# Modulation parts of a layer gathered in one PSUM bank and transposed together, ahead of attention and convolution

## The chip, the cores and the metric

One core of a Trainium2 chip runs the whole program. The metric is the device time of one execution in microseconds (us). The core has TensorE for matmuls (PE in the profile; PEld is its load of the stationary operand), VectorE (DVE), ScalarE (ACT), GpSimd (POOL) and SyncE (SP), whose queue issues the weight DMAs. TensorE writes into PSUM, eight banks of 128 partitions x 512 fp32 values.

## The reference, cut to what matters

Two transformer blocks run one after the other on 256 tokens of width 1024. The first has two layers (differential attention beside a depthwise convolution, then a feed-forward part), with 16 meta tokens ahead of the 256. The second has a gated delta rule beside dilated attention, then a mixture of 64 experts, and is modulated by a vector `c`:

```python
cs = jax.nn.silu(c)                                   # (1, 1024)
mod = (cs @ w_ada[l] + b_ada[l])[:, None, :]          # (1, 1, 6144)
sh1, sc1, gt1, sh2, sc2, gt2 = jnp.split(mod, 6, axis=-1)
h = _rms(x, g_mix[l]) * (1.0 + sc1) + sh1             # ahead of the second block's mixer
```

`mod` depends on `c` alone, so the kernel computes it during the first block. `w_ada` is 1024 x 6144 fp32, 24 MB.

## The kernel before, in words

Activations lie with features on partitions and tokens along the free axis. Dense weights pass through `weights()` (L153): a block of 1024 x 256 fp32 (1 MB) goes by one SyncE DMA into `raw`, a ring of three buffers shared by all dense weights. For the precise matmuls it is split into a high and a low fp32r part, `hi` by ScalarE (L165) and `lo` by VectorE (L166), and `mm3` (L168) issues three matmuls (L172 to L174). The modulation weights are used unsplit, straight from `raw`.

A layer of the first block (`first_block`) projects the convolution input, queries and keys, then takes the steps that the string `ORDER[l]` lists, one letter each: `s` scores and softmax (L420 to L431), `v` values (L540 to L545), `a` attention (L453 to L478), `c` convolution, `p` modulation parts, `n` channel norm (L507 to L527), `w` a block of w_out. The string is the order in which the program writes the work down. A planner with a timeline of its own then fixes each engine's order ahead of the run: earlier steps have precedence, but a later step's instruction goes first where the planner sees the earlier ones waiting. Weight DMAs and splits get a higher precedence by `PRI`. Within an engine the fixed order is kept on the chip, and SyncE issues the weight blocks in the order in which they are written down.

The convolution has 31 taps for each of four channel groups. `TAPS` gives some of them to TensorE as matmuls with a diagonal that ScalarE writes (L487, L488), 31 taps of group 0 and 16 of group 1 in layer 0, and 16 of group 0 in layer 1. ScalarE reads that sum out of PSUM (L489) and VectorE adds the other taps (L501). The channel norm needs all four groups and yields the convolution half of `cat`, of which L527 writes the last piece. The projection by w_out first sums the attention half for `AHEAD` = 5 output blocks into five banks, then the convolution half.

PSUM banks come in three kinds: `mm` and `ax` with three buffers each and `dx` with two. The convolution sums and the modulation parts use `dx`.

The modulation is cut into 24 parts of 256 columns: 12 in layer 0, 10 in layer 1 and 2 (with weights loaded ahead into `wada`) at the end of layer 1. A part (`ada_parts`, L622) takes a `dx` bank and forms eight products, one per 128 features, with `cs` broadcast to 32 columns as stationary (L630). Their column groups run side by side: product k goes to partitions 32 (k mod 4) and on. Each fp32 product is two matmuls in the trace. ScalarE copies the 128 x 256 result (L633), two more products with a column of 1/32 turn each half into one column (L635), and VectorE adds the bias into `mod` (L636).

Of the kernel before, what the change touches and what calls it, by code (L numbers as in the profile page):

```python
# [9 lines left out]
F32 = mybir.dt.float32  # L10
# [3 lines left out]
OP = mybir.AluOpType  # L14
# [4 lines left out]
KC = D // 128  # L19
# [9 lines left out]
TAPS = (((0, 31), (1, 16)), ((0, 16),))  # L29
AHEAD = 5  # L30
PR0 = 9
ORDER = ("svacpnwwww", "svacpnwwww")


GQ, GK, GV, GZ, GB, DQ, DK, DV, GA, GBB = 0, 1024, 2048, 3072, 4096, 4112, 5648, 7184, 8720, 9744
# [74 lines left out]
class K:  # L110
# [197 lines left out]
    def first_block(s):  # L308
        nc, I, V, A, PE, SP, ap, cp = s.nc, s.I, s.V, s.A, s.PE, s.SP, s.ap, s.cp
        C, ident = dict(s.C), s.C["ident"]  # L310
# [8 lines left out]
        for k in range(KC):  # L319
            p = s.ax()  # L320
# [8 lines left out]
        for l in range(2):  # L329
# [42 lines left out]
            for i, (t0, n) in enumerate(((tq, nq), (0, T))):  # L372
# [3 lines left out]
                for b in range(2):  # L376
                    w = s.weights(w_in, 0, 8, 512 * i + 256 * b)
# [9 lines left out]
            q, k = qk  # L387
# [160 lines left out]
            wo = []  # L548
            for step in ORDER[l]:
                if step == "a":  # L550
# [11 lines left out]
                else:  # L562
                    s.ada_parts(ADA[l])
            h1 = s.hp.tile([128, KC, T], F32, name="h", bufs=2)
            ps = [(s.mm, s.mm, s.mm, s.dx, s.dx, s.ax)[j]() for j in range(AHEAD)]
            for j in range(AHEAD):
                for k_ in range(4):
                    s.mm3(ps[j], wo[j // 2], k_, 128 * (j % 2), cat, k_, tq, nq, k_ == 0, False)
# [30 lines left out]
            for b in range(4):  # L599
                ws = [(s.weights(I["w_down"][l], k0 * 128, nk, 256 * b), nk, k0) for k0, nk in ((0, 8), (8, 8), (16, 6))]  # L600
# [9 lines left out]
    def ada(s):  # L610

        I, V, A, ap = s.I, s.V, s.A, s.ap
        s.P2 = s.columns(ap, s.cp, (("b_ada_2", 48), ("c_2", 8), ("g_mix_2", 8), ("g_ffn_2", 8), ("final_g", 8),
                              ("gdn_norm_g_2", 1), ("dil_q_norm_g_2", 1), ("dil_k_norm_g_2", 1)), s.G, **s.scr)
        s.cs = s.cp.tile([128, KC], F32, name="cs")
        A.activation(s.cs, s.P2["c_2"], AF.Silu)
        s.sel = s.cp.tile([128, 1], F32, name="sel")
        V.memset(s.sel, 1.0 / 32)
        s.mod = s.cp.tile([128, 6, KC], F32, name="mod")
        s.nada = 0  # L620

    def ada_parts(s, n, ws=()):  # L622
        V, A, PE, ap = s.V, s.A, s.PE, s.ap
        mod = s.mod.rearrange("p a b -> p (a b)")
        for i in range(s.nada, s.nada + n):
            w = ws[i - s.nada] if ws else s.weights(s.I["w_ada_2"][0], 0, 8, 256 * i, False)
            p = s.dx()
            for k in range(KC):
                q = 32 * (k % 4)
                PE.matmul(p[q:q + 32, :256], s.cs[:, k:k + 1].to_broadcast([128, 32]), w[:, k],  # L630
                          start=(k < 4), stop=(k >= 4))
            row = ap.tile([128, 256], F32, name="adarow", **s.row)
            A.copy(row, p[:, :256])  # L633
            for j in range(2):
                PE.matmul(p[:, 256 + j:257 + j], row[:, 128 * j:128 * j + 128], s.sel, start=True, stop=True)  # L635
            V.tensor_tensor(mod[:, 2 * i:2 * i + 2], p[:, 256:258], s.P2["b_ada_2"][:, 2 * i:2 * i + 2], op=OP.add)  # L636
        s.nada += n

    def ada_ahead(s, n):

# [1053 lines left out]
```

## Time and profile before

| | us |
|---|---|
| median of 3 runs | 1670.66 |
| lowest and highest | 1669.35, 1672.37 |
| the profiled execution's own time | 1669.04 |
| its span in the trace | 1667.2 |

The profile is of one execution; its times are in us from the span's start. Layer 0's steps from scores to w_out lie at about 81 to 194 us, layer 1's at about 440 to 545, and the last two modulation parts at 735 to 741. The experts fill the time from about 1190 on. A busy TensorE may still run at a low clock: the column PEclk is the granted clock as a share of 2.4 GHz.

### The profile page before, as it was taken

What the parts mean: (1) busy time and instruction counts of PE and PEld (TensorE: products, weight loads), DVE (VectorE), ACT (ScalarE), POOL (GpSimd) and SP (SyncE); (2) the same over time, 40 slices, a digit from 0 to 9 for tenths busy, and PEclk for the clock granted to TensorE, in tenths of its full rate; (3) what the DMA queues carried; (4) which work ended last, traced back from release to release, by engine and by line L of the source; (5) the groups of instructions that cost most, each with busy time, mean ns of one, the idle gap of its engine ahead of it and who ended that gap; (6) DMA issues with size and microseconds to landing.
All of it is one profiled execution on the core that took longest, in us unless ns stands there. A gap on an engine that the chain in (4) does not pass through costs nothing.

```text
span 1667.2 us, 32866 instructions
## 1 busy us (share of the span) xinstructions
PE 1598.1 (96%) x13630; PEld 1358.0 (81%) x13630; DVE 865.5 (52%) x1764; ACT 744.5 (45%) x1492; POOL 14.4 (1%) x28
## 2 busy tenths in 40 slices
PE   7999999999999999989999999999899999999897
PEld 6966999999968999988999999999666576566463
DVE  6685766646987666458656654553422221222122
ACT  5376644445347544455856856643322211112121
POOL 2000000000000000000000000000000000000000
PEclk9999999999999999999999999999899999999999
DMA  8408655555466555754343342666799999999995
GB/s 249 140 26 274 194 179 174 172 172 174 130 203 192 176 189 171 234 167 140 114 128 102 102 129 89 233 191 223 285 365 421 420 419 420 420 420 420 420 420 243
DMA packets 209959, 389.29 MB, mean 234 GB/s; under 512 B 8855, under 2 KB 183313, under 8 KB 184977
## 3 DMA queue, kind: packets, MB, share of 16 engines
q1 hardware_dynamic: 209104, 386.66, 64.0%
q8 instruction: 108, 1.77, 0.5%
q0 software_dynamic: 704, 0.51, 0.3%
q14 instruction: 43, 0.34, 0.1%
HBM read 386.10 MB, written 1.05 MB: 232 GB/s over the span
## 4 chain that ended last, share of the span: by engine, by line
PE 76%; DMA 14%; ACT 5%; DVE 4%; issue 1%; SPq 0%; DVEq 0%; ACTq 0%
PE mm L172 14%; PE mm L173 14%; PE mm L174 14%; PE pm L1508 6%; DMA we<-in_w_exp_up 6%; PE pm L1534 4%; DMA we<-in_w_exp_down 3%; DMA we<-in_w_exp_gate 2%; PE pm L1472 2%; PE dx L488 2%; PE mm L195 2%; PE mm L196 1%; PE mm L197 1%; ACT hi L165 1%; DMA raw<-in_w_out 1%; PE dx L630 1%
## 5 line engine op out<-in xcount | busy, mean ns | idle before, releaser
L166 DVE TENSOR_TENSOR lo<-raw,hi 128x1024 fp32r<-128x1024 f32 (+2 forms) x300 | 347.9, 1192 | 144.2 <-ACT hi L165 142.9
L165 ACT CAST hi<-raw 128x1024 fp32r<-128x1024 f32 (+2 forms) x300 | 292.7, 1024 | 271.0 <-PE mm L173 150.5
L172 PE MATMUL mm<-xh,hi 128*128 128x272 f32 (+1 forms) x1008 | 288.1, 288 | 0.0
L173 PE MATMUL mm<-xl,hi 128*128 128x272 f32 (+1 forms) x1008 | 287.8, 286 | 0.0
L174 PE MATMUL mm<-xh,lo 128*128 128x272 f32 (+1 forms) x1008 | 286.6, 286 | 0.0
L1508 PE MATMUL pm<-we,xT 128*32 128x256 f32 (+2 forms) x2048 | 195.9, 392 | 8.4 <-DMA we<-in_w_exp_up 5.8
L173 PEld LDWEIGHTS mm<-xl,hi 128*128 128x128 f32 x1008 | 189.7, 188 | 0.9
L174 PEld LDWEIGHTS mm<-xh,lo 128*128 128x128 f32 x1008 | 189.4, 188 | 0.5
L172 PEld LDWEIGHTS mm<-xh,hi 128*128 128x128 f32 x1008 | 188.5, 188 | 0.7
L1508 PEld LDWEIGHTS pm<-we,xT 128*32 128x32 f32 (+2 forms) x2048 | 122.2, 129 | 76.0 <-DMA we<-in_w_exp_up 7.9
L173 PE MATMUL mm<-bigb,hi 128*128 128x256 f32 (+1 forms) x512 | 148.3, 290 | 0.1
L172 PE MATMUL mm<-hh,hi 128*128 128x256 f32 x384 | 110.6, 291 | 7.2 <-ACT hh L704 4.2
L1534 PE MATMUL pm<-we,hT 128*32 128x512 f32 (+2 forms) x512 | 112.5, 605 | 0.1
L173 PE MATMUL mm<-hl,hi 128*128 128x256 f32 x384 | 109.5, 286 | 0.7 <-DVE hl L705 0.7
L174 PE MATMUL mm<-hh,lo 128*128 128x256 f32 x384 | 108.4, 285 | 0.0
L1519 DVE SCALAR_TENSOR_TENSOR hp<-sil,cs,pm 128x256 f32<-128x256 f32 x26 | 17.6, 676 | 168.5 <-ACT sil L1517 168.5
L174 PE MATMUL mm<-biga,lo 128*128 128x272 f32 (+1 forms) x352 | 101.4, 288 | 0.0
L172 PE MATMUL mm<-biga,hi 128*128 128x272 f32 (+1 forms) x352 | 100.6, 286 | 0.0
L173 PEld LDWEIGHTS mm<-bigb,hi 128*128 128x128 f32 x512 | 97.5, 191 | 0.8 <-DVE bigb L478 0.3
L1539 DVE TENSOR_TENSOR y<-pm,gt 128x512 f32<-128x512 f32 x52 | 35.9, 689 | 119.5 <-PE pm L1534 119.5
L1517 ACT ACTIVATE sil<-pm 128x256 f32<-128x256 f32 x26 | 10.0, 384 | 175.2 <-PE pm L1508 175.2
L195 PE MATMUL mm<-hi,hh 128*128 128x256 f32 x288 | 85.8, 298 | 2.0 <-DVE cacc L861 2.0
(541 smaller groups left out, 3089.7 us busy)
## 6 DMA issues: line engine op xcount, KB each, us to landing
we<-in_w_exp_gate SPq DMA_DIRECT2D x64, 1024.0 KB, 19.6
we<-in_w_exp_up SPq DMA_DIRECT2D x64, 1024.0 KB, 19.8
we<-in_w_exp_down SPq DMA_DIRECT2D x64, 1024.0 KB, 19.7
raw<-in_w_in SPq DMA_DIRECT2D x62, 1024.0 KB, 5.3
raw<-in_w_gate_up SPq DMA_DIRECT2D x44, 1024.0 KB, 5.1
raw<-in_w_ada SPq DMA_DIRECT2D x22, 1024.0 KB, 6.0
raw<-in_w_down SPq DMA_DIRECT2D x16, 1024.0 KB, 5.1
raw<-in_w_out SPq DMA_DIRECT2D x12, 1024.0 KB, 6.7
```

What stands on the lines that cost most here:

```text
L165: s.A.copy(hi[:, a:b], raw[:, a:b])
L166: s.V.tensor_tensor(lo[:, a:b], raw[:, a:b], hi[:, a:b].bitcast(F32), op=OP.subtract)
L172: s.PE.matmul(ps[:, :n], a, xh, start=start, stop=False)
L173: s.PE.matmul(ps[:, :n], a, xl, start=False, stop=False)
L174: s.PE.matmul(ps[:, :n], b, xh, start=False, stop=stop)
L195: s.PE.matmul(p[:, :256], xh, w[0][:, k], start=(k == 0), stop=False)
L488: PE.matmul(p[:, :nq], dg, z[:, c, tq + j:tq + j + nq], start=(j == 0), stop=(j == n - 1))
L1472: s.PE.matmul(p[:, 256 * kk:256 * kk + 256], s.ht[h][:, i, k + kk], oh[:, i], start=(i == 0 and h == 0), stop=(i == 1 and h == 1))
L1508: mm = PE.matmul(gu[sg, 256 * m:256 * m + 256], xT[:, k, o + sg.start:o + sg.stop], w[m][:, k], start=(k == 0), stop=(k == 7))
L1519: V.scalar_tensor_tensor(hp.rearrange("p k q -> p q k"), sil.rearrange("p (q k) -> p q k", k=2), cs, gu[:, 256:].rearrange("p (q k) -> p q ...
L1534: PE.matmul(py[sg], hT[:, k, sg], w[2][:, k, 512 * j:512 * j + 512], start=(k == 0), stop=(k == 1))
L1539: V.tensor_tensor(y, py, s.gt2[:, 512 * j:512 * j + 512], op=OP.mult)
```

## The change: what it does

The order string puts the parts after the values and ahead of attention and convolution. All parts of one call of `ada_parts` go into the same columns of one bank. The stationary is now a 32-column window of a tile `one` that is zero except for its middle column, which holds `cs`: shifted by the part's number i, it puts the part's result in row i of each group of 32 partitions and adds zero to the other rows. After the last part the bank is copied once. Two products with `sel`, four stacked 32 x 32 identities, sum the four partition groups and transpose, so that column i holds part i, and one addition writes all parts of the call. One of the five banks of w_out's first sums changes from `dx` to `ax`.

```diff
-ORDER = ("svacpnwwww", "svacpnwwww")
+ORDER = ("svpacnwwww", "svpacnwwww")
...
-            ps = [(s.mm, s.mm, s.mm, s.dx, s.dx, s.ax)[j]() for j in range(AHEAD)]
+            ps = [(s.mm, s.mm, s.mm, s.dx, s.ax, s.ax)[j]() for j in range(AHEAD)]
...
-        s.sel = s.cp.tile([128, 1], F32, name="sel")
-        V.memset(s.sel, 1.0 / 32)
+        s.one = ap.tile([128, KC, 63], F32, name="one")
+        V.memset(s.one, 0.0)
+        A.copy(s.one[:, :, 31], s.cs)
+        s.sel = ap.tile([128, 32], F32, name="sel")
+        V.tensor_reduce(s.sel, s.C["ident"].rearrange("p (g i) -> p i g", g=4), axis=mybir.AxisListType.X, op=OP.add)
...
     def ada_parts(s, n, ws=()):
         V, A, PE, ap = s.V, s.A, s.PE, s.ap
-        mod = s.mod.rearrange("p a b -> p (a b)")
-        for i in range(s.nada, s.nada + n):
-            w = ws[i - s.nada] if ws else s.weights(s.I["w_ada_2"][0], 0, 8, 256 * i, False)
-            p = s.dx()
+        i0, i1 = s.nada, s.nada + n
+        p = s.dx()
+        for i in range(i0, i1):
+            w = ws[i - i0] if ws else s.weights(s.I["w_ada_2"][0], 0, 8, 256 * i, False)
             for k in range(KC):
                 q = 32 * (k % 4)
-                PE.matmul(p[q:q + 32, :256], s.cs[:, k:k + 1].to_broadcast([128, 32]), w[:, k],
-                          start=(k < 4), stop=(k >= 4))
-            row = ap.tile([128, 256], F32, name="adarow", **s.row)
-            A.copy(row, p[:, :256])
-            for j in range(2):
-                PE.matmul(p[:, 256 + j:257 + j], row[:, 128 * j:128 * j + 128], s.sel, start=True, stop=True)
-            V.tensor_tensor(mod[:, 2 * i:2 * i + 2], p[:, 256:258], s.P2["b_ada_2"][:, 2 * i:2 * i + 2], op=OP.add)
-        s.nada += n
+                PE.matmul(p[q:q + 32, :256], s.one[:, k, 31 - i:63 - i], w[:, k], start=(i == i0 and k < 4),
+                          stop=(i == i1 - 1 and k >= 4))
+        row = ap.tile([128, 256], F32, name="adarow", **s.row)
+        A.copy(row, p[:, :256])
+        for j in range(2):
+            PE.matmul(p[:, 256 + 32 * j:288 + 32 * j], row[:, 128 * j:128 * j + 128], s.sel, start=True, stop=True)
+        mod, bias = (t.rearrange("p (i j) -> p i j", j=2)[:, i0:i1]
+                     for t in (s.mod.rearrange("p a b -> p (a b)"), s.P2["b_ada_2"]))
+        V.tensor_tensor(mod, p[:, 256:320].rearrange("p (j i) -> p i j", j=2)[:, i0:i1], bias, op=OP.add)
+        s.nada = i1
```

## Rows read from the trace of the kernel before

**Rows 1.** The page's busy line: time, share of the span, instructions.

```profile
PE 1598.1 (96%) x13630; PEld 1358.0 (81%) x13630; DVE 865.5 (52%) x1764; ACT 744.5 (45%) x1492; POOL 14.4 (1%) x28
```

**Rows 2.** Stretches: length, busy PE, PEld, DVE, ACT, POOL, clock, DMA share, GB/s.

```profile
86.00:116.00 30.00, 30.00 (x131) 18.66 (x129) 25.16 (x111) 19.40 (x70) 0.00 (x0) 1.00 0.00 1
131.00:158.00 27.00, 26.71 (x238) 18.43 (x242) 15.20 (x41) 12.92 (x43) 0.00 (x0) 1.00 0.84 272
158.00:165.00 7.00, 4.77 (x41) 2.93 (x34) 3.07 (x9) 5.40 (x9) 0.00 (x0) 0.65 1.07 342
165.00:171.00 6.00, 6.00 (x28) 5.69 (x28) 5.68 (x8) 6.00 (x11) 0.00 (x0) 0.55 0.86 274
...
455.00:470.00 15.00, 15.00 (x109) 13.20 (x108) 14.16 (x48) 3.01 (x11) 0.00 (x0) 1.00 0.00 1
470.00:500.00 30.00, 26.57 (x250) 15.99 (x249) 24.51 (x99) 15.80 (x53) 1.10 (x2) 1.00 0.89 280
500.00:511.00 11.00, 9.69 (x49) 7.84 (x49) 9.13 (x14) 8.61 (x13) 0.00 (x0) 0.84 1.04 327
511.00:524.00 13.00, 10.66 (x75) 9.31 (x76) 8.80 (x18) 10.29 (x27) 0.00 (x0) 1.00 0.39 129
```

**Rows 3.** Waits of SyncE, 81 to 165 us: total, times, longest.

```profile
SPq L158 <- PE dx L630: 84.0, 11, 47.1
```

**Rows 4.** Chain of waits, both layers: start, length, what.

```profile
156.25 7.34 DMA raw<-in_w_out
...
498.59 9.92 DMA raw<-in_w_out
```

**Rows 5.** Tile `adarow`, the one-column matmuls: count, ns least/median/most, first and last start.

```profile
L635 PE MATMUL dx<-sel,adarow x96: 165/250/374, 120.2 to 740.4; 128*128 128x1 f32 x96
```

**Rows 6.** Timeline of TensorE, layer 0: start, length, what, idle before.

```profile
116.80 1.07 PE L630 MATMUL dx<-raw,cs 128*32 128x256 f32 x16
117.80 1.19 PE L488 MATMUL dx<-biga,dg 128*128 128x272 f32 x4
...
133.47 0.95 PE L635 MATMUL dx<-sel,adarow 128*128 128x1 f32 x8
...
135.76 2.98 PE L461 MATMUL mm<-biga,at 128*128 128x128 f32 x14
...
160.74 1.93 PE L630 MATMUL dx<-raw,cs 128*32 128x256 f32 x16 [1.99 <-DMA raw<-in_w_ada]
162.60 1.87 PE L635 MATMUL dx<-sel,adarow 128*128 128x1 f32 x8
164.71 0.59 PE L172 MATMUL mm<-bigb,hi 128*128 128x272 f32 x1 [0.24 <-ACT hi L165]
```

**Rows 7.** Timelines of ScalarE and VectorE in both layers, same columns.

```profile
83.52 0.21 ACT L616 ACTIVATE cs<-pc_b_ada 128x8 f32<-128x8 f32 x1
...
130.60 0.46 ACT L489 ACTIVATE biga<-dx,pc_norm_g 128x272 f32<-128x272 f32 x1
...
134.85 4.26 DVE L501 SCALAR_TENSOR_TENSOR biga<-biga,cw 128x272 f32<-128x272 f32 x8
...
167.67 0.43 DVE L527 SCALAR_TENSOR_TENSOR bigb<-biga,bigb 128x272 fp32r<-128x272 f32 x1
...
490.26 0.16 DVE L636 TENSOR_TENSOR mod<-dx,pc_b_ada 128x2 f32<-128x2 f32 x1 [2.23 <-PE dx L635]
...
500.48 0.47 DVE L501 SCALAR_TENSOR_TENSOR biga<-biga,cw 128x256 f32<-128x256 f32 x1
...
520.81 0.42 DVE L527 SCALAR_TENSOR_TENSOR bigb<-biga,bigb 128x256 fp32r<-128x256 f32 x1
```

**Rows 8.** Timeline of TensorE, layer 1, same columns.

```profile
441.65 0.62 PE L630 MATMUL dx<-raw,cs 128*32 128x256 f32 x2
...
451.88 0.64 PE L630 MATMUL dx<-raw,cs 128*32 128x256 f32 x8
...
471.64 0.63 PE L630 MATMUL dx<-raw,cs 128*32 128x256 f32 x6
```

## The prediction

> **What bounds the kernel now.** I read the page's busy line first: TensorE is busy for 96% of the span [rows 1], so a stage gets shorter if work leaves TensorE, if TensorE stops waiting, or if its clock rises. The table by stretch comes second [rows 2]. In layer 0, from 86 to 116 us, TensorE is busy all 30 us at full clock while DMA moves 1 GB/s; from 131 to 165 DMA runs at 272 to 342 GB/s, and TensorE falls to 4.77 us busy of 7 at clock 0.65, then 0.55. Layer 1 has the same shape: 1 GB/s from 455 to 470, 280 to 500, clock 0.84 from 500 to 511. So the 1 MB weight blocks stand still while there is room and crowd where the stage ends.
>
> Why they stand still is in the SyncE waits [rows 3]: the weight queue waited 84.0 us in all, once 47.1, for TensorE's modulation matmuls. The ring holds three blocks. The modulation parts are planned behind attention and convolution, so their blocks lie loaded and unused. The chain of waits shows the price: it passes through the landing of w_out blocks, 7.34 us in layer 0 and 9.92 in layer 1 [rows 4]. These come late because w_out follows the modulation blocks in one queue.
>
> **The change part by part.** *Transposes.* Each part now ends in two calls which are four matmuls of one column, because fp32 goes in two passes: 96 in all [rows 5]. Eight in a row, two parts, last 0.95 us [rows 6]; a length runs some 0.07 us into the next start (1.07 at 116.80, next at 117.80), so a part's four hold 0.44 us; I take 0.45, and 24 parts cost 10.8. Afterwards there are three groups, 12 matmuls. A 32-column form with this 128x128 stationary is not in the trace. From below the one-column slot bounds it, 0.11 us; from above the 128-column one, 0.21 (14 in 2.98 us at 135.76) [rows 6]. That is 1.3 to 2.5 us; I take 1.4, since the load of the stationary is the same as with one column. Saved: 9.4 us (8.3 to 9.5), as 4.9, 4.0 and 0.4 in layer 0, layer 1 and the last two parts. In the two layers TensorE is full around it, so it counts whole.
>
> *The rows.* The 16 matmuls of a part keep their number and shape; the stationary is a 32-column window of a zero tile instead of a broadcast column, same size, and I cost it at nothing. A part takes 1.00 us (116.80 to 117.80) [rows 6], 24.0 us before and after. On ScalarE 24 copies become 3, on VectorE 24 additions become 3. In layer 1 that also takes away stalls of VectorE: the addition at 490.26 waited 2.23 us with convolution taps queued behind it [rows 7].
>
> *The move.* The order of weight loads does not change: values, modulation, w_out. What changes is when a block is used up. `cs` exists at 83.5 us [rows 7], so the three loaded blocks can go from 85 to 88, and nine more stream through a ring that never stands still. At 272 GB/s for a share of 0.84 [rows 2] a full queue gives 324 GB/s, 3.2 us for 1.05 MB: nine take 29 us, and the last part runs at about 118 instead of 160.74 [rows 6]. Behind them SyncE issues w_out some 40 us before it does now, so neither w_out wait of [rows 4] should remain. The convolution's and the scores' matmuls move back by up to ten parts, 10 us, on TensorE.
>
> *What that gives at the stage's end.* In layer 0 the recoverable loss up to 171 us is: the 1.99 us DMA wait; the last part and its transposes at half speed (1.93 for 1.07, 1.87 for 0.95), 1.8 us; gaps of 0.29 us in the window from 131 and 0.24 at 164.71; and w_out's matmuls from 165 to 171 at clock 0.55 [rows 2, 6], 2.7 us. Together 7.0. Layer 1: idle 3.43 + 1.31 + 2.34 us of the three windows from 470 to 524, and 16% of 11 us of clock, 1.8; together 8.9 [rows 2]. I don't take all of it. With the modulation gone from the end, nothing fills TensorE between the steps of attention and of the channel norm. In layer 0 convolution taps on TensorE end at 130.6 (ScalarE starts reading the bank then), VectorE's at 139.1, and the first normed tile is ready at 168.1, 29 us later [rows 7]. Layer 1 needs 20 us for this chain (500.9 to 521.2) [rows 7]. If layer 0's taps slip by 10 us and its chain shrinks to 20, w_out's second half starts as late as now and most of the 7.0 is lost; if the chain shrinks further, most is kept. I take 4 of 7.0 in layer 0, and 3 of 8.9 in layer 1, where VectorE is busy 24.5 of 30 us from 470 to 500 [rows 2] and must now do w_out's casts amid its taps.
>
> *Fragments.* The planner fits a part's matmuls in between others. Two alone last 0.62 us, eight 0.64, six 0.63 [rows 8], 16 last 1.07 [rows 6]: a cut costs 0.1 to 0.5 us. Among the dense matmuls of queries and values more parts will be cut; eight cuts at 0.25 make 2 us lost (0 to 5, the upper end with ten cuts at 0.5).
>
> The Trainium skill, "TensorEngine Tiling (Array Packing)", section Key Properties, says that changing the tiling mode drains TensorE, where changing the tile within a mode doesn't. The 128x32 fragments agree: two cost as much as eight. By this rule alone the move only adds switches, and the sum would be the transposes' 9.4 less the fragments; by the stretch table it also gives back waits.
>
> *Additions.* A memset, one strided copy and one reduction, once, near 83 us; TensorE has the matmuls of the values and scores to do meanwhile, so nothing; uncovered it would be some 0.7 us, three times the 0.21 us that `cs` takes [rows 7]. The fifth partial sum of w_out moves to a bank of the three-bank kind, free by then: nothing.
>
> *Sum.* 9.4 + 4 + 3 - 2 = 14.4 us, off the profiled execution's 1669.04 (span 1667.2 and 1.8 around it). I shade it to 13.7, since the planner reorders everything around, so 1655.3; the median of the three runs lies 1.6 above the profiled one, and the prediction is **1657**. All that follows waits for the layers' results, the experts' loads too, since their buffers are those that the mixer frees; so the gain is carried to the end.
>
> **Rivals.** *A: only TensorE work is saved.* The stage ends wait on attention and channel norm instead of on DMA. For it: the chains of 29 and 20 us; against it: much of layer 0's chain is TensorE's queue filled with modulation parts. 9.4 less 2 to 4 us: 1664.
>
> *B: cut to pieces.* If all 22 parts are cut as layer 1's first is now (2, 8 and 6: 0.62 + 0.64 + 0.63, less 0.21 of overlap, for 1.00 [rows 8]), that costs 22 x 0.68 = 15 us and leaves 1 of the 16.4 us ahead of fragments: 1669. Against it: a part becomes ready all at once, when its block lands, and those of layer 0 run mostly whole now, as the 16 at 116.80 and 160.74 [rows 6].
>
> *C: the held bank (slower).* A group now holds one of only two `dx` banks from its first to its last part. In layer 0 the convolution's second channel group takes the same bank, so its 16 taps can't begin before the last addition has read it; then come 15 taps on VectorE (8 in 4.26 us [rows 7], so 8 us) and the chain. Today TensorE's taps end at 130.6. With layer 1's chain of 20 us they may end 9 us later before w_out's second half waits longer than now; since they take some 8 us themselves, it decides when the bank comes free later than about 131. A release at 150 puts their end at 158, VectorE's at 166, the first normed tile at 186 instead of 168: 18 us lost against 9.4 saved. If the planner leaves the parts spread as today, to 164 us, it is 32 us against 9.4: 1693. For it: the parts are paced by DMA, and fall behind the scores in order. Against it: 118 us as worked out above. I price it by the release at 150: 1679.
>
> *D: it does not move.* If planned starts stay where they were since SyncE's queue decides, only the transposes go: 1661, inside A's reach.
>
> **How the numbers follow.** Forecast 62%, with its own range 1650 to 1664; A and D 17%; B 8%; C 13%. A change of under 0.2%, 3.3 us, can't be told from none here. Faster takes the forecast and most of A and D: 0.74. Same: the rest of these and most of B, 0.11. Slower: C and what of B comes out dearer, 0.15. The range runs from 1648 (all of both stages' loss given back, 9.4 + 7.0 + 8.9 less 3) to 1671 (all of B, and the mild end of C).
>
> **What would show it.** Right: one-column matmuls gone, 12 of 32 columns in at most 2.5 us; DMA above 200 GB/s between 86 and 116 us; SyncE's long wait for the modulation matmuls gone; the last modulation matmul of layer 0 before 125; w_out's first matmul at 153 to 158 rather than 164.7, and its DMA out of the chain. Wrong: TensorE waiting for `in_w_ada` in many places; the second group of convolution taps after 145; many fragments; or a low clock again ahead of w_out.

## The result and the profile after: 1.4% slower

The changed kernel takes 1693.87 us (median of 4 runs, 1690.04 to 1697.08) against 1670.54 us for the kernel before on the same chip. The ratio is 1.014 (95% interval 1.0119 to 1.0161). The forecast was 1657 us with 74% for faster: the sign is wrong. The profiled execution, the fastest of the four, took 1690.04 us, with a span of 1687.9.

The page's busy line after, against [rows 1]:

```profile
PE 1598.3 (95%) x13546; PEld 1354.3 (80%) x13546; DVE 864.4 (51%) x1744; ACT 741.7 (44%) x1474; POOL 14.5 (1%) x28
```

TensorE has 84 matmuls less (96 one-column ones became 12) and is busy as long as before: 1598.3 us against 1598.1. Its mean granted clock is 0.979 instead of 0.984; half a per cent of 1598 us is 8 us, about what the matmuls saved (an estimate).

The stretches of [rows 2] after, same columns:

```profile
86.00:116.00 30.00, 30.00 (x223) 18.02 (x222) 26.07 (x111) 14.40 (x53) 0.00 (x0) 1.00 0.66 212
131.00:158.00 27.00, 20.43 (x114) 14.21 (x113) 15.34 (x29) 20.93 (x58) 0.00 (x0) 0.92 0.60 197
...
470.00:500.00 30.00, 30.00 (x236) 16.61 (x235) 24.79 (x97) 13.60 (x49) 0.00 (x0) 1.00 0.76 245
500.00:511.00 11.00, 3.06 (x18) 2.22 (x18) 9.29 (x17) 9.37 (x18) 0.00 (x0) 0.74 0.97 310
511.00:524.00 13.00, 10.53 (x39) 8.16 (x39) 6.80 (x15) 3.90 (x8) 0.00 (x0) 0.56 0.42 143
```

The transfers did move: 212 GB/s from 86 to 116 us instead of 1. But TensorE, which was busy 26.71 of 27 us from 131 on, is now busy 20.43, and in layer 1 it works 3.06 of the 11 us from 500 on. Behind that gap its clock is low, 0.56 from 511 to 524.

SyncE's waits from 81 to 165 us, against [rows 3], and the tile `adarow`, against [rows 5]:

```profile
SPq L158 <- PE dx L634: 49.8, 11, 19.6
```
```profile
L639 PE MATMUL dx<-sel,adarow x12: 190/276/297, 136.1 to 753.9; 128*128 128x32 f32 x12
```

The timeline of TensorE after, layer 0, against [rows 6] (start, length, what, idle before):

```profile
131.45 1.07 PE L634 MATMUL dx<-raw,one 128*32 128x256 f32 x16
136.05 0.53 PE L639 MATMUL dx<-sel,adarow 128*128 128x32 f32 x4
...
149.48 3.40 PE L461 MATMUL mm<-biga,at 16*128 16x128 f32 x16
156.63 1.08 PE L474 MATMUL mm<-blob,osb 128*128 128x128 f32 x4 [3.76 <-DVE osb L470]
...
168.46 2.10 PE L515 MATMUL ax<-sq,blob 128*128 128x272 f32 x8 [2.36 <-ACT sq L514]
170.39 0.60 PE L474 MATMUL mm<-blob,osb 128*128 128x128 f32 x4
171.77 0.52 PE L172 MATMUL mm<-bigb,hi 128*128 128x272 f32 x2 [0.78 <-ACT bigb L477]
```

The last part's matmuls end at 132.5, the transposes are 0.53 us for four, and w_out starts at 171.77 instead of 164.71. In between TensorE waits for one attention tile to go from its square sums over ScalarE and VectorE to `osb`: 3.76 us. The same step before, not shown yet:

```profile
137.84 0.90 PE L461 MATMUL mm<-biga,at 16*128 16x128 f32 x4
138.68 1.06 PE L630 MATMUL dx<-raw,cs 128*32 128x256 f32 x14
139.67 0.61 PE L635 MATMUL dx<-sel,adarow 128*128 128x1 f32 x4
140.21 1.48 PE L630 MATMUL dx<-raw,cs 128*32 128x256 f32 x18
141.62 0.61 PE L635 MATMUL dx<-sel,adarow 128*128 128x1 f32 x4
142.09 1.62 PE L507 MATMUL ax<-biga,blob 128*128 128x272 f32 x6
143.54 0.60 PE L474 MATMUL mm<-blob,osb 128*128 128x128 f32 x4
```

Between the same two steps of attention (L461, L474) stood two modulation parts with their transposes and six matmuls of the channel norm (L507), and TensorE never waited. In the change the norm can't fill the gap either, because its convolution is late. ScalarE reads the second group's sum at 149.59 in the change, at 130.60 before [rows 7]:

```profile
149.59 0.49 ACT L489 ACTIVATE biga<-dx,pc_norm_g 128x272 f32<-128x272 f32 x1
```

The last attention tile comes late with them: its transposes, which w_out needs, start at 170.39 in the change, behind the norm's late L515. Before they started at 156.58 (TensorE of before):

```profile
156.58 0.64 PE L474 MATMUL mm<-blob,osb 128*128 128x128 f32 x4
```

**Where the time went.** I read marks off VectorE's timeline: the ends of the first score maximum (82.3 us before), of the last addition into `h1` in layer 0 (195.0) and layer 1 (542.5), of the mixer's first group's output (921.4) and of the last copy of the result (1658.6). The changed kernel reaches them 2.5, 7.2, 14.0, 24.3 and 20.9 us later. The first 2.5 are not the change's: every later profile has 1.1 to 3.0 there, the second experiment's with the setup of before too. So layer 0 loses 4.7 us, layer 1 6.8, the way through the mixer's first group, whose program the diff does not touch, 10.3; what follows gives 3.4 back.

### The profile page after: what moved, and what is told of

Its sections match the earlier page's. It is cut to its first block, busy times and chain, and to the rows that moved or that the text cites. A ratio compares the mean times of both kernels' runs of the same rounds, so it can differ in the third digit from the quotient of the medians.

```text
span 1687.9 us, 32609 instructions
## 1 busy us (share of the span) xinstructions
PE 1598.3 (95%) x13546; PEld 1354.3 (80%) x13546; DVE 864.4 (51%) x1744; ACT 741.7 (44%) x1474; POOL 14.5 (1%) x28
## 4 chain that ended last, share of the span: by engine, by line
PE 79%; DMA 9%; ACT 6%; DVE 4%; issue 1%; SPq 0%; DVEq 0%; ACTq 0%
PE mm L173 14%; PE mm L174 14%; PE mm L172 14%; PE pm L1514 8%; PE pm L1540 4%; DMA we<-in_w_exp_up 4%; DMA we<-in_w_exp_down 3%; PE pm L1478 2%; PE dx L488 2%; PE mm L195 2%; PE dx L634 2%; PE mm L196 1%; PE mm L197 1%; ACT hi L165 1%; DMA we<-in_w_exp_gate 1%; PE ax L420 1%
## 5 line engine op out<-in xcount | busy, mean ns | idle before, releaser
L166 DVE TENSOR_TENSOR lo<-raw,hi 128x1024 fp32r<-128x1024 f32 (+2 forms) x300 | 348.0, 1191 | 151.9 <-ACT hi L165 150.5
L165 ACT CAST hi<-raw 128x1024 fp32r<-128x1024 f32 (+2 forms) x300 | 292.9, 1025 | 275.6 <-PE mm L173 157.0
```

Of the source, the lines that this page charges most:

```text
L165: s.A.copy(hi[:, a:b], raw[:, a:b])
L166: s.V.tensor_tensor(lo[:, a:b], raw[:, a:b], hi[:, a:b].bitcast(F32), op=OP.subtract)
```

## The experiments

Each time is a median beside runs of the kernel before on the same chip (1668.7 to 1670.6 us). "Marks" are the delays of the profiled execution at the five marks; they come from one execution each, and the first one alone scatters by 2 us.

| kernel | time, us | ratio (95%) | marks, us |
|---|---|---|---|
| e1 gathered, old place | 1698.74 | 1.0165 (1.0140 to 1.0190) | 2.2, 13.6, 16.9, 25.8, 26.9 |
| e2 moved, not gathered | 1714.96 | 1.0271 (1.0237 to 1.0305) | 1.7, 15.8, 31.4, 43.8, 43.1 |
| e3 other bank | 1692.66 | 1.0138 (1.0107 to 1.0169) | 2.1, 8.1, 13.2, 22.2, 22.6 |
| e4 convolution first | 1692.96 | 1.0132 (1.0105 to 1.0158) | 2.1, 14.2, 13.2, 22.2, 23.8 |
| e5 last two own | 1682.96 | 1.0098 (1.0069 to 1.0126) | 2.2, 6.9, 14.3, 13.7, 13.9 |
| e6 e1, casts held | 1681.37 | 1.0084 (1.0059 to 1.0109) | 2.2, 3.0, 1.9, 8.2, 6.5 |
| e7 change, casts held | 1706.02 | 1.0225 (1.0208 to 1.0242) | 1.6, 11.3, 30.7, 38.5, 35.4 |
| e8 pairs, old place | 1679.01 | 1.0065 (1.0044 to 1.0087) | 2.5, 0.7, -0.1, 9.0, 7.2 |
| e9 pairs, mixer as before | 1669.75 | 1.0010 (0.9997 to 1.0023) | 3.0, 1.1, 2.8, 3.9, 1.3 |
| e10 threes, mixer as before | 1674.64 | 1.0028 (1.0012 to 1.0043) | 2.4, 2.8, 3.8, 4.9, 6.4 |
| e11 four ahead, casts held | 1683.65 | 1.0092 (1.0074 to 1.0110) | 1.1, 6.8, 12.2, 13.5, 14.6 |
| e12 no transposes | 1720.24 | not read | 1.3, 2.2, 0.0, 11.4, - |
| e13 filler added | 1695.74 | 1.0151 (1.0131 to 1.0170) | 2.3, 10.0, 17.0, 29.0, 30.2 |
| e14 casts held, layer 1 | 1684.99 | 1.0093 (1.0077 to 1.0110) | 1.8, 6.4, 8.0, 19.3, 16.1 |
| e15 four ahead, casts free | 1683.07 | 1.0085 (1.0066 to 1.0104) | 2.5, 4.4, 13.6, 13.9, 13.9 |
| e16 only last two gathered | 1684.98 | 1.0094 (1.0077 to 1.0110) | 1.8, 1.1, 1.6, 10.4, 12.1 |
| e17 e5 and e14 together | 1679.47 | 1.0050 (1.0033 to 1.0067) | 1.8, 12.4, 14.3, 15.2, 12.1 |

### First round: which half, which bank

**e1**, the change with the parts in their old place; **e2**, before with only the move; **e4**, the change with the convolution ahead of the parts:

```
e1: ORDER = ("svacpnwwww", "svacpnwwww")
e2: ORDER = ("svpacnwwww", "svpacnwwww")    # in the kernel before
e4: ORDER = ("svcpanwwww", "svcpanwwww")
```

> The changed kernel with the order string of before (parts behind attention and convolution); the gathering in one bank stays. Theory 1 (precedence): parts written ahead of the convolution push its TensorE taps back and starve VectorE's taps and the channel norm; the gathering alone only takes the one-column matmuls away, so about 1661 us (1656 to 1667), faster than before. Theory 2 (held bank): the same here, since the convolution takes its banks first, 1661. Theory 3 (the gathering itself costs, because one late read-out holds a bank and ends the parts in one lump): slower than before, 1675 or more.

> The kernel before with the new order string; every part keeps its own bank and its own transposes. Theory 1: as slow as the change or slower by the transposes, 1690 to 1705. Theory 2: no bank is held, so the second group of convolution taps is not kept waiting and little of the 23 us is left: 1665 to 1675. Theory 3: at most 1672.

> The changed kernel with the order scores, values, convolution, parts, attention. Theory 1: the convolution's TensorE taps go back to about their old place (first sum read near 115 us, second near 131), the norm's chain ends earlier than in the changed kernel and the loss in both layers goes: 1655 to 1668. Theory 2: the same. Theory 3: still above 1680.

**e3**, layer 0's second group of convolution taps takes another bank: `p = s.ax() if (l, c) == (0, 1) else s.dx()`.

> The changed kernel, with the second convolution group of layer 0 summed in a bank of the three-bank kind, so that it need not wait for the modulation's bank. Theory 1: no change beyond 4 us from the changed kernel, 1688 to 1696; the first group's sum is still read near 138 us. Theory 2: the second group starts earlier and layer 0 gives back its 5 to 7 us, 1685 or less, with ScalarE reading the second sum before 140 us instead of 149.6. Theory 3: no change.

e3 leaves the time as it is, and its second sum is read at 149.00, 0.6 us before the change's: the held bank is not the cause. e1 and e4 miss what T1 gave them (times near or under before's); e2 has T1's sign and is dearer than it said. e2, one half alone, is dearer than both together, and e1, the other, is no cheaper, so neither T1 nor T3 can be the whole. e1 shows a wait that none of the three theories had (TensorE, ScalarE, VectorE of e1, layer 0):

```profile
176.83 1.09 PE L474 MATMUL mm<-blob,osb 128*128 128x128 f32 x4 [12.46 <-DVE osb L470]
```
```profile
169.16 1.99 ACT L165 CAST hi<-raw 128x1024 fp32r<-128x1024 f32 x2 [2.21 <-DMA raw<-in_w_out]
```
```profile
170.12 0.17 DVE L202 RECIPROCAL oss<-oss 128x4 f32<-128x4 f32 x1
170.24 2.36 DVE L166 TENSOR_TENSOR lo<-raw,hi 128x1024 fp32r<-128x1024 f32 x2
...
172.59 0.16 DVE L468 TENSOR_TENSOR oss<-oss,st 128x4 f32<-128x4 f32 x1
...
175.99 0.69 DVE L470 TENSOR_TENSOR osb<-mm,oss 128x512 f32<-128x512 f32 x1
```

The planner put w_out's splits (L165 on ScalarE, L166 on VectorE; I call them casts) ahead of the last attention tile. On the chip the third block lands late, ScalarE waits for it, VectorE for ScalarE, and `osb` stands behind them in VectorE's queue. In before the first of these casts on VectorE starts at 164.69, after the last `osb`. e4 has the same wait in layer 0 (12.4 us); in the change it stands in layer 1 (TensorE, ScalarE, VectorE of the change):

```profile
513.47 1.11 PE L474 MATMUL mm<-blob,osb 128*128 128x128 f32 x4 [10.40 <-DVE osb L470]
```
```profile
505.02 1.99 ACT L165 CAST hi<-raw 128x1024 fp32r<-128x1024 f32 x2 [0.36 <-DMA raw<-in_w_out]
507.03 1.28 ACT L201 ACT_TABLE_LOAD   x1
```
```profile
508.77 0.17 DVE L202 RECIPROCAL oss<-oss 128x4 f32<-128x4 f32 x1
509.59 1.23 DVE L166 TENSOR_TENSOR lo<-raw,hi 128x1024 fp32r<-128x1024 f32 x1 [0.65 <-ACT hi L165]
...
511.13 1.22 DVE L166 TENSOR_TENSOR lo<-raw,hi 128x1024 fp32r<-128x1024 f32 x1
512.26 0.15 DVE L468 TENSOR_TENSOR oss<-oss,st 128x4 f32<-128x4 f32 x1
...
512.73 0.68 DVE L470 TENSOR_TENSOR osb<-mm,oss 128x512 f32<-128x512 f32 x1
```

From the reciprocal at 508.77 to `osb` 4 us pass, of which two casts take 2.45 and the wait for one of them 0.65; four more casts ran from 502.71 on.

### Second round: the mixer's order, and the casts

**e5**, the change, but the last two parts (ahead of the mixer) go the old way (`ada_group` is the changed code, `ada_each` the old):

```
+        (s.ada_group if (1, 1, 0)[ADA.index(n)] else s.ada_each)(n, ws)
```

> The change, but the last two modulation parts (those ahead of the mixer) each keep a bank and transposes of their own, as before. In both layers every engine's planned order stays that of the change; in the mixer it returns to that of before (in the change VectorE and ScalarE have some 38 instructions there in another order, though the mixer's program is the same). Theory M, the mixer's 10 us come from the planner laying the mixer out differently once the last two parts are gathered: the mixer's first group ends 14 us after before's instead of 24, and the time is 1681 to 1686 us. Rival N, the mixer's loss is carried in from the layers (clock, buffers, transfers that stand elsewhere): no change, 1691 to 1696.

M held: the mixer's mark falls from 24.3 to 13.7, the layers' marks stay. The same 141 us of the mixer in before, in the change and in e5 (columns as in [rows 2]), and one of TensorE's waits in the mixer's first 190 us (total, times, longest), first in the change, then in e5:

```profile
759.00:900.00 141.00, 137.24 (x1698) 132.42 (x1696) 92.18 (x185) 90.39 (x203) 1.38 (x1) 0.99 0.42 128
```
```profile
773.00:914.00 141.00, 130.68 (x1620) 125.61 (x1621) 85.56 (x172) 88.67 (x196) 1.38 (x1) 0.98 0.39 126
```
```profile
773.00:914.00 141.00, 137.38 (x1698) 132.60 (x1698) 92.17 (x185) 90.18 (x203) 1.38 (x1) 0.99 0.41 129
```
```profile
PE mm L172 <- DVE cacc L867: 4.0, 2, 3.6
```
```profile
PE mm L172 <- DVE cacc L890: 1.2, 1, 1.2
```

**e6**, e1 with the casts of the first w_out blocks queued behind the last attention tile; **e7**, the change with them queued behind the norm's squares (ScalarE) and second multiplication (VectorE):

```
+                    with s.tc.issue_after(held['a'].ins), s.tc.issue_after(held['av'].ins):   # e7: 'n', 'nv'
                         wo.append(s.weights(I["w_out"][l], 0, 8, 256 * len(wo)))
```

> The gathered parts behind attention and convolution (first experiment, 1698.7 us), and ScalarE's and VectorE's casts of the first w_out blocks are queued behind the last attention tile on their engines. Theory Q, what cost 14 us in layer 0 there is the planner's queue: it put w_out's casts ahead of the last attention tile, and the blocks land too late, so TensorE waits 12.5 us for osb behind them: layer 0's last h1 comes at most 7 us after before's instead of 13.6, layer 1's at most 10 instead of 16.9, time 1688 to 1694. Rival T3, gathering in itself costs (parts paced by their landing instead of by banks): h1 stays at +12 or more in layer 0 and the time at 1697 to 1702.

> The change, with w_out's casts queued behind the channel norm's squares (ScalarE) and its second multiplication (VectorE), where before had them. Theory Q: the casts that run at 132 to 142 us amid the convolution hold up the stationaries and taps; without them layer 0's last convolution tap comes 8 to 14 us after before's instead of 19.4, the last h1 at most 4 instead of 7.2, and the time is 1684 to 1690. Rival T1, precedence alone (the parts ahead push the convolution's and attention's matmuls back, casts or not): the tap stays at +17 or more and the time at 1691 to 1697. A third way: casts that late cost TensorE a wait of their own ahead of w_out, and the time rises above 1697.

In e6 the 12.46 us wait is 1.0, and 10.6 us of layer 0's 13.6 go: Q holds for e1, by more than expected. e7 came out the third way. The first wait for `osb` in layer 1 fell from 10.40 to 4.91 us, but all six casts now stand in one piece ahead of the second one (ScalarE, then TensorE of e7):

```profile
527.59 5.77 ACT L165 CAST hi<-raw 128x1024 fp32r<-128x1024 f32 x6
```
```profile
536.40 1.09 PE L474 MATMUL mm<-blob,osb 128*128 128x128 f32 x4 [7.94 <-DVE osb L470]
```

My place for them was ahead of the last attention tile, so e7 doesn't say what casts behind it would give.

**e8**, parts in the old place, gathered two by two (`for i in range(0, n, 2): s.ada_group(...)`), old bank for the fifth partial sum.

> Parts stand where they stood before and are gathered two by two (12 groups of two parts, 48 transposing matmuls instead of 96), so banks still pace them and the planner leaves w_out's casts behind attention in layer 0. Theory Q: layer 0's last h1 comes within 2 us of before's, layer 1's within 4, and only the mixer's 10 us are lost: 1673 to 1681. Rival T3, gathering costs in itself, less with fewer parts in a bank: between before and the gathered version, 1684 to 1692.

The two layers end as before, the mixer loses its 9: Q and M hold. Half of the transposes are gone, some 4.4 us of TensorE by the prediction's slots, and from the first score to layer 1's end 2.6 us of it show (marks 2.5 to -0.1). In layer 0 TensorE waits instead (TensorE's waits, layer 0; then ScalarE):

```profile
PE mm L172 <- ACT hi L165: 3.7, 1, 3.7
```
```profile
161.12 1.28 ACT L521 ACT_TABLE_LOAD   x1
...
164.45 1.98 ACT L165 CAST hi<-raw 128x1024 fp32r<-128x1024 f32 x2
```

That wait is ScalarE's and not the transfer's: the first w_out block has landed at 161.9, and its cast stands behind 3.3 us of the norm's work.

### Third round: is TensorE's work on the path?

**e9**, pairs, last two own, casts held as in e6; **e10**, threes, last two own, casts free; **e12**, before without the transposes (`V.tensor_tensor(mod[...], row[:, 0:2], ...)`).

> Pairs in the old place as in the eighth experiment, the last two parts each on their own, and w_out's casts queued behind the last attention tile; so planned, the mixer's order is again that of before (VectorE's and ScalarE's lists agree but for two instructions). Theory M: the 8 to 9 us that the pairs lost in the mixer go, and 1667 to 1673 us are left. Theory D, in layer 0 the stage's end waits for w_out's blocks, which the queue of modulation blocks delays, so TensorE's saved transposes turn into a wait for them: no better than before, 1668 to 1673. The prediction's first step, TensorE is full and each microsecond saved there counts whole: 1661 to 1666.

> As the last one, but groups of three parts (32 transposing matmuls in the layers instead of 88) and no queueing of the casts; the mixer's planned order is wholly that of before, and in layer 0 the planner puts two of w_out's casts on ScalarE ahead of the last attention tile's output. Theories M and D: 1667 to 1675, within 5 us of the one with pairs. The prediction's first step: 1659 to 1665, better than pairs.

> Before, with the 96 one-column transposing matmuls left out: VectorE adds the bias to two elements of the copied row instead (the modulation's numbers are then other ones). The planned mixer is that of the change. Theory D: TensorE's 9.4 us are not on the path: the last h1 of layer 0 and of layer 1 stay within 2.5 us of before's, and with the mixer's 9 to 10 us the time is 1677 to 1683. The prediction's first step: the last h1 comes 4 to 5 us earlier in layer 0 and 8 to 9 in layer 1, and the time is 1669 to 1673.

e9 is as fast as before and no faster; e10 is 0.3% slower. In e12 the layers end 2.2 and 0.0 us after before's although 96 matmuls are gone; counted from the first score, 1.3 us of their 9 show. The chain of waits in e12 runs in both layers through the landing of a w_out block (start, length):

```profile
156.62 5.14 DMA raw<-in_w_out
...
494.17 8.47 DMA raw<-in_w_out
```

D holds, the prediction's first step falls. e12's total is not read and misses what was expected: with other modulation numbers the router sends other tokens to the experts, and TensorE runs 13654 matmuls where 13630 less 96 would be 13534.

**e11**, threes, four parts of each layer ahead and the rest behind (`ORDER = ("svpacpnwwww",) * 2`), casts held as in e6; **e15**, the same with the casts left to the planner.

> Threes, with four parts of each layer (a group of three and one) ahead of attention and convolution and the others behind them, w_out's casts queued behind the last attention tile, the last two parts on their own (the mixer's order is that of before). Theory D: the weight queue starts 30 us earlier, w_out lands earlier, and eight and six parts are left to fill TensorE at the stage's end: layer 0's last h1 2 to 6 us before before's, time 1660 to 1667. Theory T1: parts ahead push attention and convolution back by about 1 us each and that is lost at the stage's end: 1674 to 1684.

> Four parts of each layer ahead, threes, the last two on their own, as in the eleventh experiment, but w_out's casts stand where the planner puts them; the mixer's order is that of before. Theory Q (the queueing cost the eleventh its time: TensorE waited 5.3 us there for the norm behind casts in layer 0): 1669 to 1676. Theory F (parts ahead take away the filler at the stage's end and push attention back, held casts or not): 1677 to 1685.

D missed in e11 and Q in e15: four parts ahead cost 1% with the casts held or free, as T1 and F had it. The time alone doesn't show F's reason, though: most of e15's loss stands in layer 1 (4.4 to 13.6), where VectorE again has six casts ahead of `osb` and TensorE waits 12.6 us for it. Freeing the casts gave layer 0 2.4 us (6.8 to 4.4) and the whole nothing.

### Fourth round: the gap at the stage's end

**e13**, the change plus 12 empty parts in layer 0 behind the convolution:

```
+                        for k_ in range(KC):        # 12 times
+                            PE.matmul(p[q_:q_ + 32, :256], s.one[:, k_, 20:52], z[:, k_ % 4, tq:tq + 256], ...)
```

> The change, with 12 empty parts in layer 0 behind the convolution: the 16 matmuls of a part each (192 in all, some 12 us of TensorE), with a constant window as stationary, convolution data as moving operand and a result that nobody reads; no transfers. The planner fits them between attention's and the convolution's steps; the rest of both layers keeps the change's order but for five VectorE instructions, the mixer gets that of the first experiment (1 to 2 us dearer). Theory F, with the parts gone ahead TensorE stands idle 10.8 of the 44 us from 131 to 175 because nothing fills the steps of attention and norm: the 12 us go into that idle time, layer 0's last h1 comes at most 5 us after the change's, time 1693 to 1699 us. Rival, the prediction's: TensorE is full and all work counts: 11 to 12 us later, 1703 to 1708.

Twelve microseconds of work put in cost layer 0 2.8 us (7.2 to 10.0). TensorE from 131 to 175 us in the change, then in e13, columns as in [rows 2]:

```profile
131.00:175.00 44.00, 33.24 (x177) 24.16 (x176) 24.13 (x47) 28.83 (x78) 0.00 (x0) 0.91 0.37 121
```
```profile
131.00:175.00 44.00, 41.28 (x355) 25.80 (x353) 20.01 (x40) 26.55 (x75) 0.00 (x0) 1.00 0.38 121
```

178 matmuls more fit into the same 44 us, and TensorE is busy 8.0 us longer there. The clock is 1.00 instead of 0.91, which gave back some of the rest; how much was not separated. F holds.

**e14**, the change with the casts held in layer 1 alone, as in e6; **e16**, before with only the last two parts gathered (`(0, 0, 1)` in e5's line); **e17**, e5 and e14 together.

> The change, with w_out's casts queued behind the last attention tile in layer 1 alone; layer 0 and the mixer keep the change's order. In the change TensorE waits 10.4 us in layer 1 for osb, and VectorE does six casts of w_out (7.3 us) ahead of it. Theory Q: that wait falls to 6 us or less, layer 1 loses at most 3 us against before instead of 6.8 (from layer 0's last h1 to layer 1's), time 1688 to 1691. Rival, the casts only move and hold up something else by as much: 1692 to 1697.

> Before, with one part of the change alone: the last two parts, ahead of the mixer, share a bank and are transposed once (4 matmuls fewer, one copy and one addition fewer). Both layers keep before's planned order but for one VectorE instruction; the mixer's order differs in 63 VectorE and 53 ScalarE instructions, as in the first experiment. Theory M: this alone costs the mixer 10 to 12 us, with the layers within 1.5 us of before's: 1679 to 1683. Rival, the mixer is dearer only after layers that end otherwise: 1667 to 1672.

> The change with both single remedies at once: w_out's casts behind the last attention tile in layer 1, and the last two parts on their own (the mixer's order is before's but for two instructions). Theories F, Q and M are separate and add up: the 5 to 7 us of layer 1 and the 10 of the mixer both go, 1673 to 1677, and what is left against before is layer 0's 5 us at the stage's end. Rival, they share a cause and do not add: 1680 to 1684.

In e14 layer 1 loses 1.6 us instead of 6.8, and TensorE's longest wait for `osb` is 4.9 us: Q holds in the change, and the time is 3 us below what I had expected. e16 pays the mixer's price with nothing else changed: marks 1.6 at layer 1's `h1` and 10.4 in the mixer, 0.9% for gathering two parts; M holds, 2 us dearer than expected. e17 lands at 1679.5, above the 1673 to 1677 of pure addition. Its marks show both remedies whole: layer 1 loses 1.9 us and the way through the mixer's first group 0.9. Its fastest run is 1675.73; the profiled one, 1681.21, lost 6 us in layer 0 in another way (last section).

## Why the prediction was wrong, by its steps

*Transposes.* The size was right: 12 matmuls, 0.53 to 0.63 us for four, 9 us of TensorE saved. The failed step is "in the two layers TensorE is full around it, so it counts whole". e12 takes all 96 away, and 1.3 us of it reach layer 1's end. A window that is nearly full (26.71 of 27 us [rows 2]) is not a path: at the stage's end TensorE is busy with modulation parts while w_out's blocks come through the queue behind them. Take work away, and it waits for what is last then: in e12 for w_out's blocks, in e8 3.7 us for ScalarE, which has the norm's work ahead of the first cast.

*The move.* All its signs in the transfers came true: 212 GB/s where 1 was, SyncE's longest wait 19.6 us instead of 47.1, w_out out of the chain at that place. The step that failed is what it gives at the stage's end: +4 and +3 us were taken, 4.7 and 6.8 were lost. It let the convolution's matmuls slip by up to 10 us; they slipped by 19.0 (149.59 for 130.60). The chain from VectorE's last tap to the first normed tile did shrink, to 18.5 us (160.7 to 179.2), from 26.8 before: [rows 7] stops one tap short, the last ends at 141.3 and not at 139.1. So the tile came 11 us late. Attention slipped too: its last transposes came 13.8 us later, and w_out, whose blocks were long there, waited for them. The prediction said that nothing would fill TensorE between the steps of attention and norm, and priced it by a chain that might shrink to 20 us. It should have counted the steps: the parts were the filler, and before them TensorE had no room (46.32 of 47 us busy from 84 to 131 before, 47.00 after). e13 shows the gap: 12 us of work fit in for 2.8, with the clock's help.

*Casts.* That VectorE "must now do w_out's casts amid its taps" stood in the prediction for layer 1 as a reason to shade the gain. It was the larger part of layer 1's loss, 5.2 of 6.8 us (e14). An early weight block is work for ScalarE and VectorE at once, and the planner, which gives such splits precedence, placed it ahead of attention's chain.

*The carried gain.* "All that follows waits for the layers' results [...] so the gain is carried to the end" left out that the planner lays everything out anew. The mixer's order changed in 38 VectorE instructions and cost 10.3 us, the largest item; e5 and e16 show that gathering the last two parts, priced at 0.4 us of gain, is enough to do it. It isn't the only way: e2 and e12 don't gather them, yet by the trace VectorE's order in the mixer differs from the change's in three or four instructions only, and the same way costs them 12.4 and 11.4 us. Every run with that order, or all but a few instructions of it, pays 6.3 to 12.4 us there, the six with the order of before (e5, e9, e10, e11, e15, e17) at most 1.3.

*The last part of layer 0* was put at 118 us, it ran at 131.45: the blocks came at 212 GB/s where 324 were taken, and the parts stand in TensorE's queue among scores, values and taps. The bank that they hold meanwhile is not what costs (e3).

*Rivals.* C, the slow one, had the right sign and the wrong mechanism: e3 moves the taps to another bank and stays at 1.0138. That its dearer form says 1693, what was measured, is luck. Of A's saving (9.4 us of TensorE) 1.3 us show in e12; e8, with half of it, shows 2.6. B's cutting didn't come: the trace has 16 pieces in layer 0 instead of 11 and 13 in layer 1 instead of 12, six more where the prediction took eight cuts. What these cost was not tried alone.

What stays open: how layer 0's 4.7 us divide between missing filler and the casts that run on ScalarE from 131.94 to 141.73, since e7 moved them to a bad place. That these are on the path is shown by the change's chain of waits (start, length), which has three of them:

```profile
136.60 0.94 ACT hi L165
...
139.82 1.91 ACT hi L165 x2
```

Open, too, is what e2, the move without gathering, loses beyond the change in the layers, and why 3.4 us came back behind the mixer's first group. No version tried beats the kernel before; e9 equals it.

## What to carry to other kernels

Work of a nearly full engine is only worth its time if nothing else is due at the same moment: look for what is due next (here a weight block or a cast) before counting it. Independent work near the end of a latency chain is filler, and moving it to where the engine is full loses it twice. Where a planner lays out the queues, hold its new order against the old one over the whole program, also where the program is unchanged: a small edit moved 10 us in a part it doesn't touch.

## What the runs showed of the hardware

After one and the same gap the clock does not stay low equally long in every run. e14 and e17 have the same order in layer 0 (but for one instruction of the setup) and the same 3.8 us wait for `osb` ahead of 157 us. The granted clock falls in both. First e14, then e17, columns as in [rows 2]:

```profile
150.00:158.00 8.00, 4.24 (x21) 3.17 (x21) 6.23 (x16) 2.49 (x10) 0.00 (x0) 0.67 0.00 0
158.00:165.00 7.00, 7.00 (x39) 5.42 (x37) 2.09 (x4) 1.87 (x4) 0.00 (x0) 0.89 0.01 2
```
```profile
150.00:158.00 8.00, 4.25 (x20) 3.19 (x20) 6.07 (x15) 2.49 (x10) 0.00 (x0) 0.61 0.00 0
158.00:165.00 7.00, 7.00 (x24) 5.22 (x24) 2.06 (x4) 1.75 (x3) 0.00 (x0) 0.50 0.01 2
165.00:171.00 6.00, 4.99 (x15) 3.42 (x14) 0.05 (x1) 1.88 (x10) 0.00 (x0) 0.50 0.00 0
```

In e14 it rises again soon after 158; in e17 it stays at 0.50, the lower of the two levels (1.2 GHz), through 171 us although TensorE is busy all 7 us from 158 on. There 24 matmuls take the 7 us in which 39 ran, and layer 0's last `h1` comes 12.4 us late instead of 6.4. The Trainium skill, "TensorE: Matmul & The Clock Gate", section "HAM oscillation — how this bites in real kernels", tells of matmul groups that start at the low clock after each wait for data. These rows agree that a gap can cost the clock; they add that the cost of the same gap varied from one execution to another, by 6 us at the layer's end here.
